# Pool values and output gates as Strassen units of the gates' pass, with the first head's elementwise work moved beside them

## The chip, the cores and the metric

The kernel runs on one core of a Trainium2 chip. Its engines are TensorE (PE in the profile; PEld is its weight load), VectorE (DVE), ScalarE (ACT), GpSimd (POOL) and SyncE (SP, which issues most DMA transfers in order). The metric is the time of one execution in device microseconds (us).

## What is computed

One layer of a decoder trunk, 1024 tokens and 16 meta tokens ahead of them (L = 1040 rows), width 1024, in float32. Cut to what matters here:

```python
u = rmsnorm(h, mix_norm_pre)
proj = u @ w_in                      # 4608 columns
q, f_logit, i_in, g_out, v_pool, gate_a, gate_b = split(proj)   # 512 x 5, 1024 x 2
a = hgrn2(q, f_logit, i_in, g_out)   # 4 heads of 128: recurrence in chunks, then rms norm, gain, * sigmoid(g)
p = multiscale_pool(v_pool)          # 4 groups of 128: trailing mean of 2, 4, 8, 16 rows minus the row,
                                     # times a 128 x 128 matrix, times a scale
z = sigmoid(gate_a) * (a @ w_branch_hgrn) + sigmoid(gate_b) * (p @ w_branch_pool)
h = h + rmsnorm(z @ w_out)
u = rmsnorm(h, ffn_norm_pre)
gt = causal_dwconv(u @ ffn_w_gate)
h = h + rmsnorm((gelu(gt) * (u @ ffn_w_up)) @ ffn_w_down)
```

In `hgrn2`, f = lb + (1 - lb) sigmoid(f_logit), k = (1 - lb) sigmoid(-f_logit), and b is the running sum of log f in a chunk.

## The kernel before

Features lie on the 128 partitions, tokens along the free axis. Every float32 product is made of three matmuls in a reduced type (float32r): the operands are split into a high and a low part (`hi` is a cast on ScalarE, `lo = x - hi` a subtraction on VectorE or GpSimd), and high x high, high x low, low x high are added in PSUM. So each weight block is loaded, cast and subtracted ahead of use (`wsplit`, `wsplit2`, and `ahead` of the Strassen class, lines 148 to 168 and 251 to 272).

There are two ways to make an output. A **projection** (`proj_parts`, line 197) makes one block of 128 output columns of w_in: 8 blocks along the contraction, 3 chunks of tokens, 3 products, 72 matmuls. It serves F (forget logits), Q, G (output gates), PV (pool values), and with fewer blocks PP (the pool's 128 x 128 matrix), BB and BA (the two branch products, 8 each, 4 blocks along the contraction). A **Strassen unit** (class `Strassen`, line 215) makes two such blocks over the two halves of the tokens with seven products P1 to P7 instead of eight. Each product has 4 blocks along the contraction and 3 matmuls for each; four products carry two extra columns (the halo) and are split into matmuls of 258 and 256 columns, three have 512. The halves of the moving operand and their sums (`b11`, `b21`, `b22`, `t1` to `t4`) are made once, before the pass; the weights' sums are made for every unit on GpSimd (`load_unit`). Results are added up on VectorE out of four PSUM pairs and handed to `put`.

The stages in order:

1. Norms, transposes and the projection of i (v of the heads), with the order of ScalarE, VectorE and TensorE written out by hand.
2. G of heads 0 and 1 (`EARLY_G = 2`), which covers the last of the Strassen sums; the results go through a sigmoid to DRAM (`gscr`).
3. **The gates' pass**: `gates.finish()` runs eight units for the columns of gate_a and gate_b; `put_gate` adds, applies the sigmoid and stores to DRAM (`sscr`). `load_unit` is called for the unit two ahead, behind P4.
4. **The heads' stage**: the string `ORDER` names the steps: F, Q, G, PV, PP, BB, BA are projections (a and b are halves of one), `c` is a head's forget chain (`chain_f`: scale, logarithm, scan), `h` the next part of `head_steps` of a head, `sp` the pool's mean and split, `sa` the split of a finished head, `w` a weight block of the FFN split ahead of time. `head_steps` makes, for six levels (2 to 64), a tile `d` from `b` (`level_in`: a subtraction, two Exp, products with q and with k), multiplies it with itself on TensorE and copies the masked result into the score tile (`level_out`); then `qs`, `kd`, `e1`, transposes, chunk states, output, norm, and the product with the output gate. The list `POOLED` names elementwise operations that run on GpSimd instead of VectorE.
5. BB and BA interleaved with the last of the heads, then w_out, norms, the FFN (a second Strassen pass of 22 units) and the down product.

Outside the parts written by hand, a planner orders each engine's instructions by the program's order and by when it thinks their inputs and tiles are there. Most tiles of stages 1 to 4 come out of one pool of 26 slots of 1088 floats per partition (`FM_SLOTS`, `LP`), so a tile can also wait for a slot. Sixteen slots hold the Strassen sums throughout stage 3.

## Time and profile before

| | |
|---|---|
| median of 3 runs | 1330.1 us (1330.08 to 1330.35) |
| time of the profiled execution | 1330.1 us |
| its span, first to last instruction | 1328.4 us |
| granted TensorE clock | 0.998 |
| DMA, mean over the span | 173 GB/s |

In a row of busy time by stretch the first two numbers are the stretch and its length; then, for each engine, busy time and number of instructions, the granted clock, the DMA engines' busy share and what they moved in GB/s. In a row of a timeline: start, duration, engine, line, operation, output and inputs, partitions and elements. In a row of a group: line, engine, operation, names, shapes, count, then busy time and mean duration in ns, then the idle time just before these instructions and what ended it. A row of waits names who waited, for whom, the sum, the number of times and the longest.

### The profile page before, as it was taken

What the parts mean: (1) busy time and instruction counts of PE and PEld (TensorE: products, weight loads), DVE (VectorE), ACT (ScalarE), POOL (GpSimd) and SP (SyncE); (2) the same over time, 40 slices, a digit from 0 to 9 for tenths busy, and PEclk for the clock granted to TensorE, in tenths of its full rate; (3) what the DMA queues carried; (4) which work ended last, traced back from release to release, by engine and by line L of the source; (5) the groups of instructions that cost most, each with busy time, mean ns of one, the idle gap of its engine ahead of it and who ended that gap; (6) DMA issues with size and microseconds to landing.
All of it is one profiled execution on the core that took longest, in us unless ns stands there. A gap on an engine that the chain in (4) does not pass through costs nothing.

```text
span 1328.4 us, 19923 instructions
## 1 busy us (share of the span) xinstructions
PE 1317.1 (99%) x7713; PEld 1177.6 (89%) x7713; DVE 970.7 (73%) x1229; ACT 566.8 (43%) x946; POOL 440.4 (33%) x327
## 2 busy tenths in 40 slices
PE   8999999999999999999999999999999999999997
PEld 7799899999999999987898888888888888888886
DVE  6765545389968777766578999888988885455758
ACT  5553333365556575235564222322222233444443
POOL 2015421226525720061025555545555652000000
PEclk9999999999999999999999999999999999999999
DMA  7134332411011157987686776676766799666644
GB/s 272 41 110 157 124 109 99 125 50 48 19 51 35 35 170 268 350 280 257 219 300 234 183 211 188 198 205 171 178 161 142 175 246 310 215 224 223 222 174 159
DMA packets 139665, 230.38 MB, mean 173 GB/s; under 512 B 9000, under 2 KB 77196, under 8 KB 139570
## 3 DMA queue, kind: packets, MB, share of 16 engines
q1 hardware_dynamic: 127506, 204.71, 45.3%
q0 software_dynamic: 12064, 24.38, 10.8%
q8 instruction: 61, 1.00, 0.3%
q14 instruction: 34, 0.28, 0.1%
HBM read 165.56 MB, written 86.53 MB: 190 GB/s over the span
## 4 chain that ended last, share of the span: by engine, by line
PE 95%; DVE 4%; DMA 0%; ACT 0%; issue 0%; SPq 0%; DVEq 0%
PE P L311 15%; PE P L312 15%; PE P L314 15%; PE pd L188 5%; PE pd L190 5%; PE pd L189 5%; PE pm L188 2%; PE pm L189 2%; PE pm L190 2%; PE sl L695 1%; PE ppv L208 1%; PE pbb L208 1%; PE ppv L212 1%; PE pbb L209 1%; PE ppv L209 1%; PE pbb L212 1%
## 5 line engine op out<-in xcount | busy, mean ns | idle before, releaser
L312 PE MATMUL P<-v,whi 128*128 128x512 f32 (+2 forms) x408 | 140.7, 353 | 0.0
L311 PE MATMUL P<-v,whi 128*128 128x512 f32 (+2 forms) x408 | 140.7, 352 | 0.0
L314 PE MATMUL P<-v,wlo 128*128 128x512 f32 (+2 forms) x424 | 135.1, 349 | 0.0
L1535 DVE TENSOR_TENSOR rot<-wraw,rot 128x1024 fp32r<-128x1024 f32 x31 | 38.0, 1225 | 72.3 <-ACT rot L1534 72.2
L282 POOL TENSOR_TENSOR swa<-wraw,wraw 128x512 f32<-128x512 f32 x28 | 42.3, 1510 | 133.0 <-DMA wraw<-in_ffn_w_gate_dram 69.3
L311 PEld LDWEIGHTS P<-v,whi 128*128 128x128 f32 x408 | 76.7, 188 | 10.4
L312 PEld LDWEIGHTS P<-v,whi 128*128 128x128 f32 x408 | 76.6, 188 | 10.2
L314 PEld LDWEIGHTS P<-v,wlo 128*128 128x128 f32 x424 | 74.0, 188 | 10.8
L256 ACT CAST whi<-wraw 128x512 fp32r<-128x512 f32 x78 | 46.1, 618 | 87.6 <-PE P L312 64.2
L190 PE MATMUL pd<-rot 128*128 128x512 f32 x272 | 82.1, 389 | 0.0
L189 PE MATMUL pd<-rot 128*128 128x512 f32 x272 | 82.1, 389 | 0.0
L188 PE MATMUL pd<-rot 128*128 128x512 f32 x272 | 81.1, 389 | 0.1
L1534 ACT CAST rot<-wraw 128x1024 fp32r<-128x1024 f32 x31 | 32.7, 1055 | 90.8 <-PE pd L190 89.4
L256 ACT CAST whi<-swa 128x512 fp32r<-128x512 f32 x56 | 33.4, 618 | 81.9 <-PE P L312 76.2
L1463 DVE SCALAR_TENSOR_TENSOR y<-g,par,y 128x1024 f32<-128x1024 f32 x44 | 64.5, 1467 | 0.8
L257 DVE TENSOR_TENSOR wlo<-swb,whi 128x512 fp32r<-128x512 f32 x56 | 59.9, 1075 | 6.9 <-ACT whi L256 6.9
L257 DVE TENSOR_TENSOR wlo<-wraw,whi 128x512 fp32r<-128x512 f32 x74 | 62.3, 864 | 2.7 <-ACT whi L256 2.7
L256 ACT CAST whi<-swb 128x512 fp32r<-128x512 f32 x56 | 33.4, 618 | 68.6 <-PE P L312 64.2
L188 PEld LDWEIGHTS pd<-rot 128*128 128x128 f32 x272 | 51.0, 188 | 11.1 <-DVE p L1471 0.5
L189 PEld LDWEIGHTS pd<-rot 128*128 128x128 f32 x272 | 51.1, 188 | 10.6
L190 PEld LDWEIGHTS pd<-rot 128*128 128x128 f32 x272 | 51.0, 188 | 10.6
L311 PE MATMUL P<-t4h,whi 128*128 128x258 f32 (+1 forms) x196 | 57.0, 307 | 0.0
(421 smaller groups left out, 4133.0 us busy)
## 6 DMA issues: line engine op xcount, KB each, us to landing
wraw<-in_w_in_dram SPq DMA_DIRECT2D x36, 512.0 KB, 4.0
yt<-ysum SPq DMA_DIRECT2D x33, 512.0 KB, 4.5
wraw<-in_ffn_w_gate_dram SPq DMA_DIRECT2D x26, 512.0 KB, 7.3
wraw<-in_ffn_w_up_dram SPq DMA_DIRECT2D x22, 512.0 KB, 6.1
wsum<-in_ffn_w_down_dram SPq DMA_DIRECT2D x22, 512.0 KB, 9.0
wraw<-in_w_out_dram SPq DMA_DIRECT2D x18, 512.0 KB, 5.5
ysum<-ys SPq DMA_DIRECT2D x11, 768.0 KB, 7.7
sa<-sscr SPq DMA_DIRECT2D x16, 513.0 KB, 6.8
```

What stands on the lines that cost most here:

```text
L188: pe.matmul(ps, ahi, bhi, start=first, stop=False)
L189: pe.matmul(ps, ahi, blo, start=False, stop=False)
L190: pe.matmul(ps, alo, bhi, start=False, stop=last)
L256: act.copy(hi, src)
L257: (pool_e if 4 <= i < 2 * self.early else dve).tensor_tensor(lo, src, rr(hi), ALU.subtract)
L282: pool_e.tensor_tensor(s1, a21, a22, ALU.add)
L311: pe.matmul(d, whi[:, k, :], xh[:, c : c + w], start=(k == 0 and onto is None), stop=False, **go)
L312: pe.matmul(d, whi[:, k, :], xl[:, c : c + w], start=False, stop=False, **go)
L314: pe.matmul(x[:, o : o + w], wlo[:, k, :], xh[:, c : c + w], start=False, stop=(k == 3), **go)
L1463: dve.scalar_tensor_tensor(a, g[:, j : j + SEQ], cvw[:, j, m : m + 1], a, ALU.mult, ALU.add)
L1534: act.copy(hi, src)
L1535: dve.tensor_tensor(lo, src, rr(hi), ALU.subtract)
```

## The change

- **Units.** The gates' pass gets four more units: G of all heads (units 8, 9) and PV of all groups (10, 11, which carry 16 extra columns, so that all 1040 rows come out). The halves of the moving operand grow from 514 to 528 columns. The units run in the order of `GATE_RUN`; `put_gate` stores sigmoid(G) in `sscr`, and PV's result goes to a tile.
- **Pooling in the pass.** Means, split and the 128 x 128 product of a group become a generator `pool_sums`, stepped by `GSTEPS` between the pass's products; the result goes to DRAM (`pscr`) and is read again by the steps `l0` to `l3`. PP and PV jobs and `sp` are gone.
- **Heads 0 and 1.** F0, Q0, F1, Q1 run where G0 and G1 ran (`FIRST_JOBS`); their sigmoids and q go to DRAM (`hscr0`). `prepare(h)` then does a head's elementwise work, a step at a time, and stores each part. `GSTEPS` has a character for every product of the pass: p is a step of `prepare`, t of a pool task, b both. It holds 32 p or b; a head has 22 steps, so the pass takes all of head 0 and ten of head 1; the other twelve are `p1` in `ORDER`. `head_steps` of both heads reads the parts.
- **Smaller edits.** The chain does its scaling on ScalarE and k's factor 1 - lb goes into q; the scan of heads 0 and 1 is made in nine pieces; the copies of levels 32 and 64 go to ScalarE, except one (`ON_ACT`); weights of the next unit are loaded behind P6 of the one before (`soon`); BB's results are stored and read again where more than four `h` steps follow (`SPILL`); v's meta rows are read from DRAM by every head; `ORDER` and `POOLED` are new; 27 slots of 1056 instead of 26 of 1088.

```diff
-EARLY_G = 2
+FIRST_JOBS = (("F", 0), ("Q", 0), ("F", 1), ("Q", 1))
-FM_SLOTS = 26
-LP = 1088
+FM_SLOTS = 27
+LP = 1056
+GS = HEADS
+V_UNIT = KD + GS // 2
+GATE_RUN = [0, 8, 1, 3, 2, 10, 9, 4, 11, 6, 5, 7]
...
+ORDER = ("p1 p1 p1 p1 h0 F2 p1 h0 p1 h0 p1 Qa2 p1 p1 p1 p1 p1 h0 h0 c2 h1 w1 Qb2 h0 w0 Fa3 h1 h0 h2 h0 h0 h2 w4 h1 "
+         "h0 h1 h1 h2 l0 Fb3 w4 c3 h1 h0 Q3 h0 h2 h2 h1 h3 h1 w4 l1 h2 h2 l2 l3 h1 h1 w2 h3 BB0 h2 h2 h3 h2 w5 BB1 "
+         "h3 h1 BB2 h3 BB3 w5 h1 h3 BB4 h3 h2 BB5 w3 sa1 h3 h3 h3 sa0 h2 BB6 h3 h1 w5 h2 BB7 sa2 w5 h3 sa3 BA1 BA5 "
+         "BA6 BA2 BA4 h3 BA0 BA3 BA7")
+POOLED = ("e1k.0 e1k.3 kdsub.2 lk32.1 lk4.1 lq32.1 lq64.3 lq8.0 osg.2 wBA2 wBA6 wBA7 wBB2 wF0 wF3 wPP2 wPV0 wPV1 "
+          "wQ0 qsmul.1 lq2.1 wQ2 sub2.3 lk32.3 lq4.2 sub8.0 lq32.0 lk64.1 sub8.3 lk2.1 qsmul.0 sub4.2 lq8.3 lq32.3 "
+          "lk16.1 lq2.0 lk8.1 sub32.2 lf.1 lq4.3 sub4.1 e1q.2 sub2.0 qsmul.3 lq4.0 lk8.3 sub64.1 lq8.2 lq4.1 sub2.2 "
+          "lk4.2 e1k.2 e1k.1 wQ3 kdsub.1").split()
+ON_ACT = "lo32.0 lo32.1 lo64.0 lo64.1 lo32.2 lo64.2 lo64.3".split()
+SPILL_OVER = 4
+GSTEPS = "p....pp.p.....pp...p...ptp.p.p.ppp.b.p..ttttbtttb.ttbbpbbttttbttbtttbb.tbt.bt.bppt.t"
...
             self.ahead(self.lead)
+            if self.steps:
+                c, self.steps = self.steps[0], self.steps[1:]
+                if c in "tb" and self.tasks:
+                    next(self.tasks[0], None) or self.tasks.pop(0)
+                if c in "pb":
+                    self.next_step()
...
-            return (0, 512 - HN // 2 - HALO, HT) if self.halo(u) else (HALO, 0, HN)
+            e = self.extra(u)
+            return self.most - e, (HN - e) // 4 * 2 if e else 0, HN + e
...
             dve.tensor_tensor(u2, u2, self.product(u, "P6"), ALU.add)
+            if load is not None and self.soon:
+                self.load_unit(load)
...
-        dve.tensor_scalar(f, f, oml[:, h : h + 1], lb[:, h : h + 1], ALU.mult, ALU.add)
-        dve.tensor_scalar(kk, kk, oml[:, h : h + 1], None, ALU.mult)
-        dve.tensor_scalar(f2, f, LUP, 1.0, ALU.mult, ALU.min)
-        dve.tensor_scalar(f2, f2, LOG_FLOOR * LUP, None, ALU.max)
+        act.activation(f2, f, AF.Identity, scale=omlu[:, h : h + 1], bias=lbu[:, h : h + 1])
+        act.activation(f, f, AF.Identity, scale=oml[:, h : h + 1], bias=lb[:, h : h + 1])
+        yield
+        dve.tensor_scalar(f2, f2, 1.0, LOG_FLOOR * LUP, ALU.min, ALU.max)
...
+    def prepare(h):
+        f = load_part("f", h)
+        yield True
+        kk, b, f2 = load_part("kk", h), slot(L, name="b"), slot(L, name="f2")
+        for _ in chain_steps(h, kk, b, f, f2):
+            yield True
+        del f2
+        nc.sync.dma_start(hpart("f", h), f)
+        q = load_part("q", h)
...
+        for lv in LEVELS:
+            d = slot(L, name="d")
+            for _ in level_steps(h, lv, d, q, kk, b):
+                yield True
+            nc.sync.dma_start(hpart(lv, h)[:, NM:], d[:, NM:L])
+        for z in ("qs", "kd"):
+            t = slot(L, name=z)
+            for _ in (qs_steps if z == "qs" else kd_steps)(h, t, q, kk, b):
+                yield True
+            lo = NM if z == "qs" else 0
+            nc.sync.dma_start(hpart(z, h)[:, lo:], t[:, lo:L])
...
     def put_gate(u, i, h, a, b, c=None):
+        if u >= V_UNIT:
+            if (u, i) not in vps:
+                vps[u, i] = slot(L, name="vp")
...
+    def whole_gate(u, i):
+        if u >= V_UNIT:
+            gates.tasks.append(pool_sums(2 * (u - V_UNIT) + i, vps.pop((u, i))))
...
-    gates = Strassen([(WIN, c + 2 * P * j) for c in (CA, CB) for j in range(KD // 2)], range(KD), EARLY, gq,
-                     lambda u: True, put_gate, lambda u, i: None)
+    gate_units = [(WIN, c + 2 * P * j) for c, n in ((CA, KD), (CB, KD), (CG, GS), (CV, HEADS)) for j in range(n // 2)]
+    gates = Strassen(gate_units, GATE_RUN, EARLY, gq,
+                     lambda u: NM if u >= V_UNIT else HALO, put_gate, whole_gate, NM)
...
+    gates.tasks = [load_ppw()]
+    gates.soon = True
     gates.finish()
```

More of the change, by code (lines that the diff above doesn't have):

```diff
@@ L225, in trunk_kernel, with __init__ @@
         SECOND = ("P3", "P5", "P7")
-        def __init__(self, units, run, early, quarters, halo, put, whole):
+        def __init__(self, units, run, early, quarters, extra, put, whole, most=HALO):
             self.units, self.run, self.early, self.bq = units, run, early, quarters
-            self.halo, self.put, self.whole = halo, put, whole
+            self.extra, self.put, self.whole, self.most = extra, put, whole, most
+            self.tasks, self.then, self.steps = [], [], ""
             self.raws, self.sums, self.p1s, self.halves = {}, {}, {}, {}
@@ L374, in rest @@
             x4 = self.product(u, "P4")
-            if load is not None:
+            if load is not None and not self.soon:
                 self.load_unit(load)
@@ L506, in warm @@
         for _ in range(n):
[L507 removed]
+            pe.matmul(junk_bank[:, :P], ones, ident, start=True, stop=True)
     wi = []
@@ new lines, in e1_steps, with all_of @@
+    def e1_steps(h, lf, q, kk):
+        e1 = slot(SEQ, name="e1")
+        lo2, q2, k2 = (t[:, NM:].rearrange("p (b two) -> p b two", two=2)[:, :, 1] for t in (lf, q, kk))
+        act.activation(e1[:, : SEQ // 2], lo2, AF.Exp)
+        act.activation(e1[:, SEQ // 2 :], lo2, AF.Exp, scale=-1.0)
+        yield
+        eng(f"e1q.{h}").tensor_tensor(q2, q2, e1[:, : SEQ // 2], ALU.mult)
+        eng(f"e1k.{h}").tensor_tensor(k2, k2, e1[:, SEQ // 2 :], ALU.mult)
+    def all_of(steps):
+        for _ in steps:
+            pass
@@ L1123, in trunk_kernel @@
         gates.load_first(3)
+        gates.steps = GSTEPS
+        gates.then = [prepare(h) for h in EARLY_HEADS]
         for e in range(0, EARLY, 2):
@@ L1173, in trunk_kernel @@
             continue
+        if kind == "p":
+            gates.next_step()
+            continue
         if kind == "h":
+            while i in EARLY_HEADS and len(gates.then) >= len(EARLY_HEADS) - EARLY_HEADS.index(i):
+                gates.next_step()
             if i not in gens:
```

403 lines of the change are left out of this document (248 added, 155 removed), and 3 rows, old and new, of the table ORDER.

## The prediction

> **What bounds the kernel now.** I read the busy times first, then busy time by stretch, TensorE's timeline for the pace of its matmuls, and last VectorE's groups where it is fullest.
>
> ```profile
> PE 1317.1 (99%) x7713; PEld 1177.6 (89%) x7713; DVE 970.7 (73%) x1229; ACT 566.8 (43%) x946; POOL 440.4 (33%) x327
> core 0: us, PE busy (x) PEld busy (x) DVE busy (x) ACT busy (x) POOL busy (x), PEclk, DMA share, GB/s
> 66.70:89.15 22.45, 22.45 (x145) 22.44 (x144) 17.86 (x38) 11.00 (x27) 0.00 (x0) 1.00 0.44 130
> 89.15:245.90 156.75, 156.75 (x1059) 145.51 (x1058) 76.78 (x112) 56.64 (x105) 56.15 (x40) 1.00 0.36 120
> 245.90:483.40 237.50, 236.93 (x1794) 232.97 (x1792) 185.13 (x201) 138.42 (x226) 107.44 (x53) 1.00 0.16 48
> 483.40:529.60 46.20, 46.20 (x301) 45.95 (x301) 34.37 (x57) 26.21 (x37) 2.42 (x1) 1.00 0.82 279
> 529.60:581.00 51.40, 51.40 (x327) 51.40 (x326) 37.67 (x65) 14.13 (x25) 7.01 (x4) 1.00 0.90 311
> 300.00:350.00 50.00, 49.56 (x408) 48.90 (x407) 49.61 (x42) 32.19 (x52) 34.50 (x18) 1.00 0.15 43
> 800.00:1100.00 300.00, 300.00 (x1657) 261.23 (x1656) 263.09 (x297) 86.84 (x141) 165.66 (x126) 1.00 0.73 186
> ```
>
> The stretches follow the kernel: the two early G projections (66.70), the gates' pass of eight Strassen units (89.15), heads with F, Q, G, PV and PP (245.90), BB (483.40), BA (529.60 to the first w_out matmul at 581.00). TensorE is busy in all of them, at a granted clock of 1.00; over 245.90 to 483.40 it is idle for 0.57 us. So a microsecond of matmul taken away is a microsecond of span, and there is nothing else to win; but whatever makes TensorE wait is paid in full.
>
> A busy row can hide waits, so the pace itself has to be seen:
>
> ```profile
> start us, us, engine line op out<-in xcount [idle before <-releaser]
> 66.70 0.32 PE L208 MATMUL pg<-uhi,whi 128*128 128x342 f32 x1
> 66.86 0.32 PE L209 MATMUL pg<-ulo,whi 128*128 128x342 f32 x1
> ...
> 89.15 0.28 PE L311 MATMUL P<-uhi,whi 128*128 128x258 f32 x1
> 89.27 0.28 PE L312 MATMUL P<-ulo,whi 128*128 128x258 f32 x1
> ...
> 115.05 0.39 PE L311 MATMUL P<-t1h,whi 128*128 128x512 f32 x1
> 115.28 0.39 PE L312 MATMUL P<-t1l,whi 128*128 128x512 f32 x1
> ...
> 245.88 0.32 PE L208 MATMUL pf<-uhi,whi 128*128 128x348 f32 x1
> 257.34 0.32 PE L208 MATMUL pq<-uhi,whi 128*128 128x342 f32 x1
> ```
>
> The second column overlaps the next row; the distance between starts is the cost: 0.16 us for 342 columns, 0.12 for 258, 0.23 for 512. Two G projections of 72 matmuls take 89.15 - 66.70 = 22.45 us, 11.23 each (0.156 a matmul). F0, shaped like a PV projection, takes 257.34 - 245.88 = 11.46. A Strassen unit, which makes two output blocks, takes 156.75 / 8 = 19.59.
>
> **The change on TensorE.** (1) Four G projections become two units: 4 x 11.23 - 2 x 19.59 = 5.74 us less. (2) Four PV projections become two units. These carry 16 extra columns instead of 2, so in four products of seven each matmul has 264 columns, 7 more than now on average: (0.156 - 0.12) / (342 - 258) x 7 = 0.003 us, times 96 matmuls 0.29. So 4 x 11.46 - 2 x (19.59 + 0.29) = 6.08 less. (3) PP: 36 matmuls x 0.156 = 5.6 before; after, four groups of six split matmuls and three whole ones, 4 x (6 x 0.12 + 3 x 0.23) = 5.6: nothing. (4) F0, Q0, F1, Q1 only move ahead of the gates: nothing. Together **11.8 us less**.
>
> Where the stages then lie: ahead of the gates 2 x (11.46 + 11.23) = 45.4 us instead of 22.45; the gates' pass 10 x 19.59 + 2 x 19.88 + 5.6 = 241.3 instead of 156.75; after it 335.1 (245.90 to 581.00) less eight F and Q (90.8) less G2, G3 (22.45), PV (45.84) and PP (5.6), plus F2, Q2, F3, Q3 (45.4), which is 215.8. The sum falls from 514.3 to 502.5. All that follows is untouched.
>
> **Who must keep up, in the gates' pass.** By the row of 89.15 a unit needs 9.6 us of VectorE, 7.1 of ScalarE, 7.0 of GpSimd in 19.59. Twelve units need 115 of VectorE. Added: head 0's level work by the groups below (4 x 1.68 + 2 x 1.20 + 6 x 0.89 = 14.5), some 16 for its other steps and its chain, 8 for the ten steps of head 1, 18 for the pooling (below). That is 172 of 241.3 us, 71%. The FFN's Strassen pass (800:1100) runs VectorE at 263.09 / 300 = 88% without a gap on TensorE, so I cost this at 0; without that cover, the same 18 us of pooling would be the loss. DMA: 18 more transfers of half a megabyte for the two heads and 8 for pooling are some 13 MB, 55 GB/s beside 120, still under the 186 of the FFN's pass: 0. A unit's weights are now asked for behind P6 of the unit before it, five products ahead of their first use, not twelve:
>
> ```profile
> wraw<-in_w_in_dram SPq DMA_DIRECT2D x36, 512.0 KB, 4.0
> ```
>
> Five products are some 14 us, two loads land in 4.0 to 8, and the split behind them works on half of what L155 does in 1.69 us (quoted below), so about 1 us on ScalarE and 1 on VectorE, an estimate: hidden, with 4 us to spare at the least; past that, every late unit stops TensorE, which is how the queue rival would cost.
>
> ScalarE mixes Exp and Ln steps with the gates' Sigmoid, and each alternation loads a table:
>
> ```profile
> 284.15 0.16 ACT L665 COPY scm<-sm 16x4 f32<-16x4 f32 x1
> 284.35 1.28 ACT L677 ACT_TABLE_LOAD   x1
> 285.64 0.64 ACT L677 ACTIVATE d<-d 128x512 f32<-128x512 f32 x1
> ```
>
> From the end of the copy (284.31) to the next instruction is 1.33 us. Some 15 groups of Exp or Ln at two loads each are 40 us, on 12 x 7.1 for the units and about 33 for the moved activations: 158 of 241 us, hidden. The Trainium skill (ScalarE: Activation LUTs, "What ACT_TABLE_LOAD costs") puts a switch at 1283 ns and a drain of some 1380 more. The trace agrees on the load and shows no drain behind it; with it the 15 groups would be 80 us and ScalarE 82% full, still hidden.
>
> **Who must keep up, behind the gates' pass.** Here cover is taken away: 335.1 us of matmuls become 215.8, and every BA product needs all four heads, so what the heads need of VectorE must fit into 215.8 - 45.2 (eight BA at 36 x 0.157) = 170.6 us. What it needs, by groups of now:
>
> ```profile
> L675 DVE TENSOR_TENSOR d<-b 128x1024 f32<-128x1024 f32 x20 | 32.8, 1678 | 1.1 <-ACT e L743 1.1
> L680 DVE TENSOR_TENSOR d<-d,kk 128x512 f32<-128x512 f32 x20 | 17.8, 891 | 0.1
> L679 DVE TENSOR_TENSOR d<-d,q 128x512 f32<-128x512 f32 x13 | 15.6, 1203 | 0.0
> ...
> L155 DVE TENSOR_TENSOR wlo<-wraw,whi 128x1024 fp32r<-128x1024 f32 x6 | 10.1, 1687 | 0.2 <-ACT whi L154 0.2
> L896 DVE TENSOR_TENSOR sa<-sa,pba 128x342 f32<-128x342 f32 x22 | 10.1, 506 | 10.7 <-PE pba L212 9.4 <-DMA sa<-sscr 0.8 <-PE pba L190 0.5
> ...
> L632 DVE TENSOR_TENSOR_SCAN b<-keep_on,f 128x1040 f32<-128x1040 f32 x4 | 9.3, 2325 | 0.2
> L1202 DVE TENSOR_TENSOR sa<-sa,sa 128x1026 f32<-128x1026 f32 x7 | 8.6, 1232 | 0.1
> L865 DVE TENSOR_TENSOR pll<-s,plh 128x1026 fp32r<-128x1026 f32 x4 | 7.0, 1743 | 0.6 <-ACT plh L864 0.6
> L872 DVE SCALAR_TENSOR_TENSOR plo<-ppp,par,phi 128x342 fp32r<-128x342 f32 x12 | 6.3, 567 | 0.0
> ...
> L631 DVE TENSOR_TENSOR f<-f,f 128x1040 f32<-128x1040 f32 x4 | 5.0, 1242 | 4.4 <-ACT f L630 4.4
> L859 DVE SCALAR_TENSOR_TENSOR s<-s,vp 128x1026 f32<-128x1026 f32 x4 | 4.9, 1221 | 1.8 <-POOL s L847 1.8
> L624 DVE TENSOR_SCALAR f<-f,oml,lb 128x1040 f32<-128x1040 f32 x4 | 4.6, 1141 | 13.4 <-ACT f L619 13.4
> ...
> L626 DVE TENSOR_SCALAR f<-f 128x1040 f32<-128x1040 f32 x4 | 3.9, 970 | 0.0
> ...
> L704 DVE COPY sc<-sl 32x256 f32<-32x256 f32 x8 | 3.3, 415 | 5.3 <-PE sl L691 5.2
> ...
> L625 DVE TENSOR_SCALAR kk<-kk,oml 128x1040 f32<-128x1040 f32 x4 | 3.0, 752 | 0.0
> ...
> L704 DVE COPY sc<-sl 64x512 f32<-64x512 f32 x4 | 2.7, 675 | 0.1
> ```
>
> Now it is busy 185.13 + 34.37 + 37.67 = 257.2 us. What leaves: pooling 7.0 + 6.3 + 4.9 = 18.2; five of six weight splits, 8.4; of the chain three instructions of every head (to ScalarE, or merged), 4.6 + 3.0 + 3.9 = 11.5, and two heads' scan and add, (9.3 + 5.0) / 2 = 7.1; levels, where the new engine list leaves VectorE nine instructions of each kind for heads 1 (from its third level on), 2 and 3: 66.2 - 9 x (1.68 + 0.89 + 1.20) = 32.3; the copies of the two widest levels, all but two now on ScalarE, 5.2. That is 82.7 less, 174.5 left, and 18.7 of it (L896 of pba, L1202) belong to BA's own time: **156 us of VectorE in 170.6**, 91%. Small steps of head 0 that I left out would lower it. Three edits I cost at 0 here: heads 0 and 1 read their parts, the pooled values and the meta rows of v from DRAM, where the row of 245.90 shows 48 GB/s and a DMA share of 0.16 (their first reader is an h step queued behind the p steps on VectorE, and F2's matmuls cover the landing); BB's results are stored and read again; the scan of heads 0 and 1 is cut into nine pieces ahead of time.
>
> Can it run at 91% while TensorE never waits? In 300:350 it ran at 99% and TensorE lost 0.44 us; in the FFN's pass at 88% with no loss. But over the whole of 245.90 to 483.40 it ran at only 185.13 / 237.50 = 78%, since chains leave it idle. Bounds: 0 at 99%; 156 / 0.78 - 170.6 = 29.4 at 78%. I take 90%, nearer the two rows where it had work in stock, for the planner can here choose among three heads, weight splits for the FFN and BB: 156 / 0.90 - 170.6 = **2.7 us**.
>
> The profiled execution has a time of 1330.1 us, 1.7 around its span of 1328.4; the median of the runs is also 1330.1. So 1330.1 - 11.8 + 2.7 = **1321.0**.
>
> **The rivals.** *No wait at all*: 1318.3. For it, the row of 300:350; against it, 91% is more than any long stretch shows.
>
> *VectorE becomes the bound behind the gates' pass*, and the kernel is slower: at the 78% of now the heads end 29.4 us late and BA with them: 1330.1 - 11.8 + 29.4 = 1347.7. It decides once its share falls below 156 / (170.6 + 11.8) = 85.5%; there the gain is gone.
>
> *SyncE's queue in the gates' pass.* It issues in order and mostly stands waiting:
>
> ```profile
> SPq L888 <- ACT sg L887: 83.1, 25, 6.9
> SPq L275 <- DVE wlo L257: 25.5, 8, 5.2
> ```
>
> These are 108.6 of 156.75 us; behind a store that waits for its sigmoid stand the next weights. About 26 more transfers, each holding the queue for 83.1 / 25 = 3.3 us, are 86; scaled to twelve units the old waits take 163 of 241, so 8 us would not fit: 1330.1 - 11.8 + 8 = 1326.3, and with tile slots that come free later the 1330 of no change. Against it: a wait that ends because its data come costs nothing while the next weights are four products ahead.
>
> **How the numbers follow.** Forecast 0.45, its own range 1318.5 to 1326; no wait 0.25; the queue 0.15 (0.06 a smaller gain, 0.05 no change, 0.04 slower); VectorE 0.15 (0.04 no change, where its share is near the 85.5%, and 0.11 slower, mostly short of the full price). A difference under 0.2%, 2.7 us, could not be told from none. Faster: 0.45 + 0.25 + 0.06 = 0.76; same: 0.05 + 0.04 = 0.09; slower: 0.04 + 0.11 = 0.15. The range reaches from just under the case of no wait, 1317, to 1335, about half of VectorE's price.
>
> **What would show it.** Right: the stretch from the first gate product to the first pf behind it is 241 to 245 us long, TensorE has no row of idle time before P, pg is gone and ppv is P; the time from there to the first w_out matmul is 216 to 222; VectorE is near 90% up to the first pba; idle time before pba or sl names VectorE, none longer than a few us. Wrong: idle time before P released by a DMA or by wlo (the queue), or a first pba preceded by tens of us with VectorE below 85%.

## The result and the profile after

The changed kernel takes **1341.66 us** (median of 6 runs, 1339.31 to 1347.07) beside 1330.24 for the kernel before on the same chip: a ratio of 1.0088, 95% interval 1.0068 to 1.0108. The forecast was 1321.0 and faster; the range ended at 1335. Measured twice more, each time beside the kernel before, it gave 1335.28, ratio 1.0043 (1.0028 to 1.0058), and 1334.91, ratio 1.0042 (1.0029 to 1.0056). So it is slower each time, by 4 to 11 us (0.4 to 0.9%, with 1 outside the interval each time), and what makes that spread is part of the answer.

Busy time by stretch, of the profiled execution (1341.08 us, span 1339.2). The columns are those of the rows in the prediction; 67.40 is the first of the early jobs, 113.70 the first product of the gates' pass, 357.30 the first pf behind it, 541.40 the first pba, 588.40 the first w_out matmul.

```profile
core 0: us, PE busy (x) PEld busy (x) DVE busy (x) ACT busy (x) POOL busy (x), PEclk, DMA share, GB/s
67.40:113.70 46.30, 45.66 (x290) 45.38 (x288) 22.31 (x49) 20.50 (x56) 0.00 (x0) 1.00 0.44 145
113.70:357.30 243.60, 243.37 (x1620) 223.95 (x1621) 178.13 (x226) 142.13 (x204) 127.98 (x79) 1.00 0.50 162
357.30:541.40 184.10, 177.23 (x1371) 171.91 (x1370) 132.98 (x169) 112.98 (x176) 62.11 (x38) 0.95 0.81 261
541.40:588.40 47.00, 46.23 (x293) 45.67 (x292) 34.97 (x56) 14.88 (x26) 7.00 (x4) 1.00 0.81 300
357.30:588.40 231.10, 223.45 (x1662) 217.59 (x1661) 167.95 (x224) 127.86 (x201) 69.11 (x42) 0.96 0.81 269
357.30:400.00 42.70, 39.77 (x270) 38.85 (x269) 28.16 (x20) 26.73 (x39) 28.43 (x18) 0.88 1.01 320
...
371.60:381.80 10.20, 9.40 (x41) 9.40 (x42) 3.57 (x5) 6.59 (x13) 2.81 (x2) 0.50 1.06 382
381.90:450.00 68.10, 66.41 (x564) 64.82 (x563) 53.00 (x60) 46.65 (x73) 20.74 (x13) 1.00 0.83 282
450.10:456.90 6.80, 5.76 (x61) 5.61 (x62) 6.38 (x10) 6.74 (x14) 1.85 (x1) 0.50 0.96 236
```

Against the forecast's lengths, the early jobs took 46.3 us (45.4), the gates' pass 243.6 (241.3), the heads' stage 231.1 (215.8). What lies ahead grew by 0.7, and what follows, w_out to the end, from 747.4 to 750.8 (1328.4 - 581.0 and 1339.2 - 588.4). The excess is 0.7 + 0.9 + 2.3 + 15.3 + 3.4 = 22.6 us, and -11.8 + 22.6 = +10.8 is the growth of the span from 1328.4 to 1339.2. Two thirds of it sit in the heads' stage. There the row shows three things at once: TensorE idle for 231.10 - 223.45 = 7.65 us, a granted clock of 0.96, and a DMA share of 0.81 where the kernel before had 0.16 over most of the stage. Right behind the gates' pass the DMA engines are full: 1.01.

TensorE's timeline of the changed kernel shows what belongs together (start, duration, engine, line, operation, names, shapes, idle time before and what ended it):

```profile
369.04 0.63 PE L222 MATMUL pf<-uhi,wlo 128*128 128x348 f32 x3
371.14 0.25 PE L808 MATMUL sm<-rq,em 128*16 128x2 f32 x4 [1.47 <-DMA rq<-hscr]
372.40 7.09 PE L833 MATMUL sl<-r 128*128 128x64 f32 x32 [1.00 <-DMA r<-hscr]
...
380.54 0.49 PE L218 MATMUL pq<-uhi,whi 128*128 128x342 f32 x1
380.82 0.49 PE L219 MATMUL pq<-ulo,whi 128*128 128x342 f32 x1
...
382.22 0.32 PE L218 MATMUL pq<-uhi,whi 128*128 128x342 f32 x1
382.38 0.32 PE L219 MATMUL pq<-ulo,whi 128*128 128x342 f32 x1
...
447.73 1.06 PE L879 MATMUL pt<-ident,rkd 128*128 128x128 f32 x8 [0.60 <-DMA rkd<-hscr]
448.63 0.27 PE L882 MATMUL pt<-ident,rkd 128*16 128x128 f32 x1
451.14 2.97 PE L829 MATMUL sl<-d 128*32 128x32 f32 x48 [2.23 <-DVE d L757]
```

F2's matmuls run out before head 0's parts have come from DRAM: 1.47 us idle for q, 1.00 for a level. From 371.60 the clock stands at 0.50 for 10.2 us, and the pq matmuls start 0.28 us apart instead of 0.16. The second place is at 449: head 1's transposes wait for kd, then head 2's level for VectorE, and from 450.10 the clock is 0.50 again for 6.8 us. Both stretches are multiples of 3.41 us by the clock's records (10.24 and 6.83). What they cost shows beside a later execution of the same program without half clock (the row of 357:581 below): TensorE was busy there for 216.96 us, here for 223.45, so 6.5 us. With the 7.65 idle that is 14.1 of the stage's 15.3; the rest, 217.0 against 215.8, is the matmuls' own.

Of the idle time in the stage, 3.9 us end with a DMA (q, a level, kd, the pooled values) and 3.7 with VectorE or ScalarE. In two later profiles of the same program it is 3.1 and 4.2, then 1.7 and 5.2. So transfers are a part of the waiting, and the chains of elementwise work are as large a part.

Why q came late: SyncE's queue, and some of the issues with their median time from issue to landing, over 357 to 590:

```profile
360.38 4.12 SPq L691 DMA_DIRECT2D rq<-hscr  x1
364.59 0.38 SPq L691 DMA_DIRECT2D r<-hscr  x1
```

```profile
sa<-sscr SPq DMA_DIRECT2D x16, 513.0 KB, 8.5
r<-hscr SPq DMA_DIRECT2D x12, 512.0 KB, 7.1
sb<-sscr SPq DMA_DIRECT2D x7, 513.0 KB, 9.4
vh<-vscr SPq DMA_DIRECT2D x4, 512.0 KB, 8.1
```

In the kernel before, over 246 to 483, `vh` landed in a median of 5.3 us, and `sa` in 6.8 in its own full stretch; here they take 8.1 and 8.5. Not every transfer is slow: `sg` lands in 4.7. The issue of rq alone holds the queue for 4.12 us. In the two later profiles it holds it for 3.22 and 2.77, and there TensorE doesn't wait for q, only for the level behind it (1.00 and 0.74 us).

The wait for `d` at 451 is of another kind. ScalarE's timeline:

```profile
441.32 1.42 ACT L679 ACTIVATE q<-pq,oml 128x342 f32<-128x342 f32 x3 [1.46 <-PE pq L222]
442.75 1.28 ACT L939 ACT_TABLE_LOAD   x1
444.05 1.42 ACT L939 ACTIVATE rs<-ms,eps_t 128x342 f32<-128x342 f32 x3
445.49 1.28 ACT L753 ACT_TABLE_LOAD   x1
446.78 0.63 ACT L753 ACTIVATE d<-d 128x512 f32<-128x512 f32 x1
447.32 0.61 ACT L754 ACTIVATE d<-d 128x512 f32<-128x512 f32 x1
```

Head 2's Exp stands behind head 0's norm, with a table load on either side of it, 2.56 us of loads on the chain that TensorE waits for. VectorE's products follow at 447.44 and the matmul at 451.14. ScalarE idles for 1.46 us until Q3's last matmuls are done, and then works without a break: 9.72 of the 9.80 us from 441.30 to 451.10, VectorE 7.42. So for these 10 us it is full, though over the whole stage it is busy for only 127.86 of 231.10 us. No run takes the table loads or the norm out of that place, so this reading rests on the timeline.

### The profile page after: what moved, and what is told of

Its sections match the earlier page's. It is cut to its first block, busy times and chain, and to the rows that moved or that the text cites. A ratio compares the mean times of both kernels' runs of the same rounds, so it can differ in the third digit from the quotient of the medians.

```text
span 1339.2 us, 20195 instructions
## 1 busy us (share of the span) xinstructions
PE 1319.1 (98%) x7665; PEld 1166.1 (87%) x7665; DVE 991.3 (74%) x1260; ACT 610.5 (46%) x985; POOL 466.2 (35%) x348
## 2 busy tenths in 40 slices
DMA packets 149217, 277.83 MB, mean 207 GB/s; under 512 B 10536, under 2 KB 74700, under 8 KB 149122
## 3 DMA queue, kind: packets, MB, share of 16 engines
q0 software_dynamic: 12064, 24.38, 10.8%
## 4 chain that ended last, share of the span: by engine, by line
PE 88%; DMA 5%; ACT 2%; DVE 1%; issue 1%; POOL 1%; SPq 1%; DVEq 0%; POOLq 0%; ACTq 0%
PE P L322 16%; PE P L325 16%; PE P L323 16%; PE pd L198 5%; PE pd L200 5%; PE pd L199 5%; PE sl L833 2%; PE pm L199 2%; PE pm L200 2%; PE pm L198 2%; DMA wraw<-in_w_out_dram 2%; DMA sb<-sscr 1%; PE pv L199 1%; PE pv L200 1%; PE pv L198 1%
## 5 line engine op out<-in xcount | busy, mean ns | idle before, releaser
L267 ACT CAST whi<-wraw 128x512 fp32r<-128x512 f32 x90 | 53.0, 618 | 81.7 <-PE P L323 68.4
L268 DVE TENSOR_TENSOR wlo<-wraw,whi 128x512 fp32r<-128x512 f32 x86 | 80.5, 958 | 12.7 <-ACT whi L267 12.7
L293 POOL TENSOR_TENSOR swa<-wraw,wraw 128x512 f32<-128x512 f32 x32 | 50.0, 1564 | 111.2 <-DMA wraw<-in_ffn_w_gate_dram 74.6
L323 PEld LDWEIGHTS P<-v,whi 128*128 128x128 f32 x408 | 76.6, 188 | 10.3
L268 DVE TENSOR_TENSOR wlo<-swb,whi 128x512 fp32r<-128x512 f32 x64 | 71.6, 1125 | 9.0 <-ACT whi L267 9.0
L267 ACT CAST whi<-swa 128x512 fp32r<-128x512 f32 x64 | 38.1, 616 | 76.6 <-PE P L323 71.0
L322 PE MATMUL P<-uhi,whi 128*128 128x258 f32 (+2 forms) x240 | 69.0, 304 | 0.6 <-ACT q L679 0.6
L267 ACT CAST whi<-swb 128x512 fp32r<-128x512 f32 x64 | 38.2, 617 | 67.4 <-PE P L323 63.5
L323 PE MATMUL P<-ulo,whi 128*128 128x258 f32 (+2 forms) x240 | 68.9, 305 | 0.0
L322 PE MATMUL P<-t2h,whi 128*128 128x258 f32 (+2 forms) x228 | 65.3, 304 | 0.2 <-DVE sg L1022 0.2
L322 PE MATMUL P<-t4h,whi 128*128 128x258 f32 (+2 forms) x228 | 64.9, 302 | 0.1
```

The costliest lines, as they stand in the source:

```text
L267: act.copy(hi, src)
L268: (pool_e if 4 <= i < 2 * self.early else dve).tensor_tensor(lo, src, rr(hi), ALU.subtract)
L293: pool_e.tensor_tensor(s1, a21, a22, ALU.add)
L322: pe.matmul(d, whi[:, k, :], xh[:, c : c + w], start=(k == 0 and onto is None), stop=False, **go)
L323: pe.matmul(d, whi[:, k, :], xl[:, c : c + w], start=False, stop=False, **go)
```

## The experiments

The expectations call the layout of tiles A (alignment first, then the stride, A2) and the waits and transfers behind the gates' pass B. Ratios are against the kernel before on the same chip.

### Layout: slots of 1056 floats

512-column matmuls start 0.2267 us apart on average in the gates' pass of before and 0.2311 after (mean over 280 and 429 pairs of neighbours). This distance is called the pitch below. Two kernels add 64 bytes ahead of the pools, to the changed kernel and to the one before:

```diff
+    pad = const.tile([P, 16], F32, name="pad")
+    pool_e.memset(pad, 0.0)
```

> The changed kernel with one more constant tile of 64 bytes per partition, so that all large tiles lie 64 bytes further on (at multiples of 128 bytes, as in the kernel before); nothing else differs. Theory A (part of the loss is the tiles' place in memory: 512-column matmuls of the gates' pass start 0.231 us apart after the change and 0.227 before): the mean distance falls to 0.227, the gates' pass is about 2 us shorter, the whole time about 4 to 5 us, from 1341.7 to about 1337. Rival (the slower matmuls come from the added transfers or VectorE work): no change in the distance, 1341.7.

> The kernel before with the same tile of 64 bytes, which puts its large tiles 64 bytes off a multiple of 128. Theory A: its 512-column matmuls in the gates' pass go from 0.227 to about 0.231 us apart and the time rises by 4 to 5 us, to about 1334.5. Rival: 1330.2 as before.

The pitch stayed at 0.2311 and 0.2267; the times are 1336.15, ratio 1.0039 (1.0025 to 1.0052), and 1330.41, ratio 1.0000 (0.9992 to 1.0009). A shift by 64 bytes does nothing to the pitch. That the time still came out at the first expectation's 1337 is luck: the kernel with no edit gave 1335 in both later measurements. Next the stride, in the kernel before (`U0 = LP - L` follows it: the rows begin 16 floats into their part of the two large tiles, not 48):

```diff
-LP = 1088
+LP = 1056
```

> The kernel before with tile slots of 1056 instead of 1088 floats per partition, nothing else. Theory A2 (the slower 512-column matmuls come from the slots' stride, which puts rows at other places in the memory): matmuls of the gates' pass go from 0.227 to 0.231 us apart and the time rises by 4 to 5 us to about 1334.5. Rival (it comes from the added work, transfers or instructions): 0.227 and 1330.2.

1335.31 us, ratio 1.0034 (1.0021 to 1.0047), pitch 0.2301 in the gates' pass. Its stretches:

```profile
67.50:90.10 22.60, 22.60 (x146) 22.60 (x145) 17.62 (x38) 11.01 (x27) 0.00 (x0) 1.00 0.43 129
90.10:247.90 157.80, 157.80 (x1057) 145.57 (x1056) 76.50 (x112) 56.72 (x104) 55.86 (x40) 1.00 0.36 119
247.90:583.50 335.60, 334.74 (x2419) 330.23 (x2418) 257.80 (x320) 178.77 (x287) 116.04 (x58) 1.00 0.36 120
```

A full clock, the same order of work, and the span is 1333.2 instead of 1328.4. The 4.8 us are spread: 0.8 ahead of the first row, 0.15, 1.05, 0.5 in the rows, 2.3 behind. The 0.8 is a wait of 0.74 us at 7.7 that the profile of before doesn't have, while one of the changed kernel has it too (1.36 us). The other 4.0 are put down to the stride; the medians are 4.4 apart. Scaled to the longer gates' pass of the changed kernel (1.05 x 243.6 / 156.75 = 1.6 in place of 1.05) the 4.0 become some 4.6 us there, an estimate. The pitch shows it; the rows only say that TensorE is busy.

The obvious remedy is the old stride, with one slot less so that it fits:

```diff
-FM_SLOTS = 27
-LP = 1056
+FM_SLOTS = 26
+LP = 1088
```

> The changed kernel with tile slots of 1088 floats again and 26 of them, as in the kernel before; the order of the engines' work is almost the same. Theory A2 (the stride of 1056 costs some 5 us over the whole kernel): matmuls of the gates' pass 0.227 us apart, the gates' pass 241.3 us, the time about 5 us under e5's 1335.3, so about 1330.5. Rival (the 27th slot is needed): transfers are asked for later, more idle time behind the gates' pass, 1336 or more.

The pitch came back (0.2276, without eight of 428 pairs that ran at half clock), and the time went up to 1352.42, ratio 1.0156 (1.0140 to 1.0172). Its waits of TensorE and its gates' pass:

```profile
PE P L322 <- DVE plo L983: 3.5, 1, 3.5
PE sl L829 <- DVE d L757: 3.4, 1, 3.4
PE P L322 <- ACT e L779: 2.5, 1, 2.5
```

```profile
113.00:367.00 254.00, 245.46 (x1620) 226.23 (x1621) 178.82 (x226) 142.61 (x205) 129.05 (x80) 0.99 0.47 156
```

TensorE idles for 8.5 us in the pass and waits for head 0's and the pool's elementwise work. The likely reason is the missing 27th slot, without which that work can't run as far ahead. So the faster stride is bought with a slot, and here the slot is worth more. Between the two, the stride of 1088 for the two large tiles alone, which hold the high and the low part of the normed input:

```diff
-U0 = LP - L
+UP = 1088
+U0 = UP - L
...
-        return upool.tile([P, n], dtype, tag="u", name=nm(name), padded_shape=[P, KD * LP])
+        return upool.tile([P, n], dtype, tag="u", name=nm(name), padded_shape=[P, KD * UP])
```

> The changed kernel with 1088 floats per row only in the two large tiles that hold the normed input's parts, and 27 slots of 1056. If the stride of these tiles decides, the first stage's matmuls (their weights come from these tiles) are 0.227 us apart again and the time is 1 to 3 us under e5; if the slots' place decides, only those products of the gates' pass that read the large tiles change, or none.

1335.79, ratio 1.0040 (1.0028 to 1.0053); the gates' pass 242.3 us, pitch 0.2302. To take the chip out of the comparison, the changed kernel and this one ran again side by side:

> The changed kernel itself, as the base for the two runs beside it on one chip. Earlier chips gave 1.0088 and 1.0043 of the kernel before; both theories expect between these.

> Only the two large tiles of the Strassen halves at a stride of 1088 floats, 27 slots of 1056 kept. If the stride of what TensorE reads is worth what the shorter matmul pitch in that kernel's gates' pass says (243.6 down to 242.3 us, and 0.5 ahead of it), it is 1.5 to 3 us faster than the changed kernel on the same chip; if the earlier difference was the chip's or that of the half-clock stretches, less than 1 us.

1334.91, ratio 1.0042 (1.0029 to 1.0056), and 1337.03, ratio 1.0040 (1.0026 to 1.0054). The gain of 1 to 2 us that the pitch shows can't be told in the time.

### The half clock, and the waits behind the gates' pass

The changed kernel once more, with no edit:

> The changed kernel once more, so that the others are compared on one chip. Both theories: 1341.7 within 3 us, two stretches of half clock between 357 and 470 us.

1335.28, with one stretch of half clock (3.41 us) instead of two. The later run side by side (1334.91) had none in its profiled execution; its busy time by stretch, gates' pass and heads' stage:

```profile
113.60:356.90 243.30, 242.98 (x1619) 223.76 (x1620) 179.57 (x226) 142.69 (x205) 128.27 (x79) 1.00 0.50 162
357.00:581.00 224.00, 216.96 (x1663) 210.73 (x1661) 167.45 (x223) 127.38 (x201) 70.44 (x42) 1.00 0.80 277
```

The stage is 224.0 us, 7 us less than in the first profile, with nearly the same idle time (7.04). So half clock, not more waiting, makes the difference between these two. Over the 19 executions of this kernel, the eight with a mean clock of 0.997 or more average 1334.7 us, the nine at 0.994 or less 1341.7. So most of the spread between the three measurements goes with the half clock. But even the execution without any half clock has a span of 1331.9, 3.5 above before.

Can the waits be covered? First, by putting all of Q2 ahead of head 0's matmuls:

```diff
-ORDER = ("p1 p1 p1 p1 h0 F2 p1 h0 p1 h0 p1 Qa2 p1 p1 p1 p1 p1 h0 h0 c2 h1 w1 Qb2 h0 w0 Fa3 h1 h0 h2 h0 h0 h2 w4 h1 "
+ORDER = ("p1 p1 p1 p1 h0 F2 Qa2 Qb2 p1 h0 p1 h0 p1 p1 p1 p1 p1 p1 h0 h0 c2 h1 w1 h0 w0 Fa3 h1 h0 h2 h0 h0 h2 w4 h1 "
```

> The changed kernel with the whole of Q2 ahead of head 0's first matmuls, so that TensorE has 11 us of work while head 0's parts land; three p1 steps move with it. Theory B (head 0's parts come late from DRAM at the end of the gates' pass, TensorE stands 2.8 us and then runs at half clock for 10.2 us): both go, 2.8 + 5.1 = about 8 us, 1341.7 to about 1334; granted clock 1.00 from 366 to 382 us. Rival (VectorE or the engines as a whole are behind, the gap only moves): the time stays within 3 us of 1341.7.

1343.19, ratio 1.0092 (1.0079 to 1.0105), beside 1336.15 of the padded kernel on the same chip. The wait for q moved from 371 to 403 us and grew to 2.6, and the one for `d` grew from 2.2 to 5.7. The Q2 matmuls covered nothing, because the steps behind them became later as well.

Second, to keep the clock up, 15 matmuls on constants behind F2:

```diff
+        if kind == "j":
+            fill = bank("pj")
+            for _ in range(15):
+                pe.matmul(fill[:, :P], ones, ident, start=True, stop=True)
+            continue
...
-ORDER = ("p1 p1 p1 p1 h0 F2 p1 h0 ...
+ORDER = ("p1 p1 p1 p1 h0 F2 j0 p1 h0 ...
```

> The changed kernel with 15 matmuls on constants (about 3 us, result unused) between F2 and head 0's first matmuls. They end no wait. Theory C (the half clock follows from TensorE being idle for some 3 us): the clock stays at 1.00 there and the time falls by about 5 us although work was added, to about 1337. Rival (the clock drops for another reason, as the load of the other engines or of DMA): the clock drops at the same place and the time stays or rises, 1341.7 to 1345.

TensorE's timeline and stretches in that run:

```profile
369.71 3.51 PE L1339 MATMUL pj<-ident,ones 128*128 128x128 f32 x30
373.15 0.25 PE L808 MATMUL sm<-rq,em 128*16 128x2 f32 x4
373.34 3.79 PE L833 MATMUL sl<-r 128*128 128x64 f32 x32
```

```profile
369.00:382.00 13.00, 13.00 (x104) 12.86 (x103) 5.20 (x5) 9.77 (x16) 8.31 (x5) 1.00 1.05 379
441.10:454.70 13.60, 13.60 (x95) 12.94 (x95) 12.62 (x16) 10.86 (x18) 2.84 (x2) 0.50 0.70 221
```

The 32 matmuls of sl take 3.79 us instead of 7.09 and the clock is 1.00, with the DMA share as high as before. One execution doesn't show it, since other executions have no half clock here without a fill either. Over all profiles that have these steps behind F2, none of three with a fill shows half clock there, and six of twelve without do, at a DMA share of 0.99 to 1.10 over the 13 us around that place in each. So full transfers alone don't bring the half clock, and idle time is the likely cause. The fill replaces the wait and doesn't end it: the time is 1338.64, ratio 1.0055 (1.0043 to 1.0067), no better than the padded kernel's 1336.15 on the same chip, and a gap of 1.93 us at 439 is followed by 13.65 us of half clock. Filling both places, with the large tiles at 1088:

```diff
-... h0 Q3 h0 h2 h2 h1 h3 h1 ...
+... h0 Q3 h0 h2 h2 j0 h1 h3 h1 ...
```

> As the run beside it, with 15 matmuls on constants behind F2 and 15 more ahead of head 1's steps behind Q3, where TensorE waits. If idle time costs mainly through the half clock that follows it, the clock stays at 1.00 over 360 to 460 us and the kernel is 3 to 5 us faster than the one beside it, about 1331. If each wait has its own cause that comes later anyway, the half clock moves behind another gap and the time stays within 2 us or gets longer.

1339.71, ratio 1.0068 (1.0056 to 1.0080), slower than the kernel beside it (1337.03). A gap of 1.96 us at 437 names ScalarE's `rh`, and 13.65 us of half clock follow. With 26 slots of 1088, Q3 was moved four steps back in one kernel, and both fills were put into another:

```diff
-... h0 Q3 h0 h2 h2 h1 h3 h1 ...
+... h0 h0 h2 h2 h1 Q3 h3 h1 ...
```

> e9 with Q3 behind head 2's next step and one of head 1, so that its 11 us of matmuls stand where TensorE waits near 445 us. Theory B (what is left of the loss is short waits behind the gates' pass, where too little matmul work is ready, each followed by half clock): the wait and the half clock near 445 go, 3 to 6 us less than e9, to about 1326, under the kernel before. Rival (the heads are late as a whole): the wait moves to another place, same time as e9.

> e9 with 15 matmuls on constants (about 3 us each time, result unused) behind F2 and another 15 behind head 2's step after Q3. They end no wait. Theory C (idle time costs twice, by the half clock that follows): no half clock between 357 and 470 us, 2 to 5 us less than e9, about 1327. Rival: no gain, 1330 to 1334.

1359.01, ratio 1.0216 (1.0202 to 1.0230), and 1355.77, ratio 1.0188 (1.0175 to 1.0202), against 1.0156 without either edit. In each of these runs TensorE waits for the next chain instead, and none is faster than the kernel without the edit.

### Slots, transfers, VectorE, and dividing the heads

BB's results kept in slots, not stored and read again:

```diff
-SPILL_OVER = 4
+SPILL_OVER = 99
```

> The changed kernel with BB's results kept in their slots, no store to DRAM and no second load: 14 transfers of half a megabyte less between 460 and 590 us. Theory B (the transfers behind the gates' pass are what TensorE waits for): the DMA share from 460 to 588 falls, BA's stretch and the first w_out matmuls lose their waits, 2 to 4 us less, to about 1338; the gaps near 370 and 450 stay. Rival (the tile slots are the limit): the kept results hold eight slots, loads are asked for later, and the time rises above 1342.

1347.50, ratio 1.0123 (1.0110 to 1.0136). TensorE waits once for 10.3 us, and the DMA share over 460 to 540 us falls to 0.48 (its waits, then that stretch):

```profile
PE sl L829 <- POOL d L757: 10.3, 1, 10.3
```

```profile
460.00:540.00 80.00, 69.22 (x513) 67.37 (x513) 48.47 (x77) 37.09 (x57) 16.39 (x11) 0.91 0.48 152
```

Beside 1335.28 on the same chip that is 12 us more, with fewer transfers and the same work on the engines (VectorE 990.2 us, 991.3 in the first profile). So the stores of BB pay for themselves. A slot for `d` that comes free too late, as the rival had it, is not what the trace names: GpSimd's wait for `d` ends with ScalarE's Exp, and ScalarE stood still for 3.98 and 5.11 us ahead of two weight casts in front of it, first until a store of another weight was done, then until a load came. Why these are late is open.

Transfers in the other direction: eight copies of half a megabyte within DRAM at the start of the heads' stage (large tiles at 1088):

```diff
+    extra = dram.tile([8, P, TQ], F32, name="extra")
+    for i in range(8):
+        nc.sync.dma_start(extra[i], sd[14 + i % 2])
```

> e10 with eight added copies of half a megabyte from DRAM to DRAM at the start of the heads' stage (result unused), 8.4 MB read and written. At the 320 to 340 GB/s seen there they are some 13 to 25 us of transfers. Theory B: the time rises by 8 us or more, to 1344 or more, with TensorE waiting for heads' parts. Rival (transfers have room): up to 3 us more.

1349.62, ratio 1.0151 (1.0136 to 1.0166), beside 1.0040 without them (on another chip): some 15 us. TensorE's longest wait and the heads' stage in the profiled execution, the slowest of four (1353.07):

```profile
PE sm L809 <- DMA rq<-hscr: 7.2, 1, 7.2
```

```profile
355.30:601.20 245.90, 230.60 (x1662) 224.60 (x1661) 163.21 (x224) 128.22 (x201) 67.42 (x42) 0.92 0.79 270
```

They stand in front of head 0's q, whose wait grows to 7.2 us; idle time doubles to 15.3 us (6.95 without them), and 37.55 us run at half clock. Moving the FFN's weight splits, whose loads share the queue, to later places, most of them behind BB0, should then help:

```diff
-... c2 h1 w1 Qb2 h0 w0 Fa3 h1 h0 h2 h0 h0 h2 w4 h1 h0 h1 h1 h2 l0 Fb3 w4 c3 h1 h0 Q3 h0 h2 h2 h1 h3 h1 w4 l1 ...
+... c2 h1 Qb2 h0 Fa3 h1 h0 h2 h0 h0 h2 h1 h0 h1 h1 h2 l0 Fb3 c3 h1 h0 Q3 h0 h2 h2 h1 h3 h1 l1 ...
```

> e10 with the FFN's weight blocks that are split ahead of time moved behind BB0: about 7 MB of loads and stores, and 10 us of VectorE, leave the first 90 us behind the gates' pass. Theory B (the transfers there set the pace: DMA share 0.89 to 1.0): the share from 357 to 446 us falls to about 0.7, the waits near 370 and 445 shrink, the time falls by 4 us or more, to 1331 or less. Rival (chains of VectorE and ScalarE in heads 0 to 2): less than 2 us.

It doesn't: 1341.14, ratio 1.0091 (1.0074 to 1.0108). At the start of the stage it does what was expected, though the DMA share over 357 to 400 stays at 1.03: TensorE idles for 0.29 us there instead of 0.87, and the clock is 1.00 instead of 0.92. Over 400 to 440 the share falls from 0.74 to 0.58. But the waits at 440 (4.3 us for `d`) and 552 (4.4 for `sa`) name VectorE, and both are longer than without the edit (1.6 and 1.1). So the transfers ahead of head 0's parts seem to decide the wait at the start of the stage, and chains of ScalarE and VectorE the later ones.

VectorE's share itself, with 20 added sums of 512 columns (a median of 0.69 us each; VectorE is busy for 15.8 us more in the stage). The edit, and the row of the stage:

```diff
+    scr = const.tile([P, 512], F32, name="scr")
+    pool_e.memset(scr, 0.0)
+    added = []
...
+            if len(added) < 20 and "v" in heads[i]:
+                added.append(dve.tensor_tensor(scr, heads[i]["v"][:, :512], scr, ALU.add))
```

> The changed kernel with 20 added VectorE additions of 512 columns (0.7 us each, 14 us in all) behind the first 20 steps of the heads (result unused). Theory B: VectorE has room (72% busy), up to 4 us more, 1339 at most. Rival (VectorE is the bound behind the gates' pass, as one rival of the prediction had it): 10 us or more, 1345 or more.

```profile
357.60:590.40 232.80, 221.33 (x1663) 215.66 (x1661) 183.78 (x245) 128.16 (x202) 70.96 (x42) 0.98 0.78 268
```

1344.10, ratio 1.0102 (1.0087 to 1.0117). The stage is 232.8 us at 79% VectorE, with 11.5 idle. Against the 1.0042 and 1.0043 above that is some 8 us, against the first 1.0088 almost nothing, so the size is not settled; it lies between the two forecasts. A full VectorE would have cost all of the 15.8; the result fits chains with little other work in stock better, but doesn't settle it.

Last, only head 0 moved ahead (F1 and Q1 back in the stage, with an order put together by hand and not tuned):

```diff
-FIRST_JOBS = (("F", 0), ("Q", 0), ("F", 1), ("Q", 1))
+FIRST_JOBS = (("F", 0), ("Q", 0))
...
-ORDER = ("p1 p1 p1 p1 h0 F2 p1 h0 p1 h0 p1 Qa2 p1 p1 p1 p1 p1 h0 h0 c2 h1 w1 Qb2 h0 w0 Fa3 h1 h0 ...
+ORDER = ("h0 F1 h0 c1 Q1 h0 h1 h0 F2 h0 h1 c2 Qa2 Qb2 h1 w1 h0 w0 Fa3 h1 h0 ...
```

> The changed kernel with only head 0 beside the gates; F1, Q1 and head 1's work go behind the pass as in the kernel before, 26 transfers of half a megabyte less and 22.7 us more matmuls to cover VectorE, which gets some 26 us of work there. Theory B (transfers and the waits on them): DMA share from the end of the gates' pass to the first w_out matmul falls from 0.81 to about 0.65, no half clock or one short stretch of it, and the time falls to 1320 to 1328, under the kernel before. Rival (VectorE is the bound behind the pass): moving head 1's work back makes it later, the time rises to 1345 or more.

1360.83, ratio 1.0224 (1.0210 to 1.0237). The DMA share of its stage is 0.59, and it waits 8.4 us for `po <- st` and runs 37.5 us at half clock. With fewer transfers it is slower, so taking transfers away does not help when elementwise work comes back in their place; how much of the loss is the untuned order stays open.

No kernel tried was faster than the one before.

## Why the prediction was wrong

**The failed step** is "three edits I cost at 0 here", and with it two prices that have no term at all: the half clock behind a wait, and the stride. The cover named for the three edits was the row of 245.90, with 48 GB/s and a DMA share of 0.16. That is the stage as it was before the change put transfers into it and took a third of its length away. The whole kernel moves 277.83 MB instead of 230.38; from the end of the gates' pass to w_out it was 40.17 MB in 335.1 us, 120 GB/s, and is 62.88 MB in 233 us, 270 GB/s. The prediction even names what saves the first read: F2's matmuls. They cover some 12 us; the queue takes 4.12 to issue q, in the stretch where the DMA share is 1.01, and in the first profile q came 1.47 us late. Waits that end with a DMA come to 3.9 us of the stage there, and to 3.1 and 1.7 in the two later profiles. The reads were set beside the bytes of the old stage, and never turned into bytes per microsecond of the shorter one.

**The price of a wait** was missing as well. The prediction takes a stall at its length. In the first profile 7.65 us idle brought another 6.5 of half clock. The Trainium skill (TensorE: Matmul & The Clock Gate, "Part 1: The HAM clock gate") says the clock halves after an idle window of about 3.4 us and comes back after a busy one, with free-running windows. The trace agrees on the half and on the unit (10.24, 6.83 and 3.41 us), but no gap in the first profile was as long as 3.4 us. Behind F2, far less was enough in one execution and not in another of the same program, that with the large tiles at 1088: 0.84 us of idle time was followed by the first of these rows, 0.99 by the second (the stretch 371.70 to 378.50 of its two profiles).

```profile
371.70:378.50 6.80, 6.80 (x28) 6.80 (x28) 4.93 (x5) 4.50 (x7) 3.97 (x2) 0.50 1.05 390
```

```profile
371.70:378.50 6.80, 6.80 (x49) 6.80 (x49) 5.14 (x5) 4.70 (x8) 3.77 (x2) 1.00 1.03 402
```

The first made 28 matmuls in 6.80 us, the second 49. The clock's records show what differs. In each of the 20 profiles every change of the clock lies on a grid of 3.413 us, the full stretches between included (365.23, 68.27 and 880.64 us in the first profile are 107, 20 and 258 units), and the grid starts at another place in every execution. In the slow one of these two a unit began at 368.25, ahead of the gap's end at 368.70, so it held idle time and then only narrow matmuls; in the other one a unit began at 369.34, behind the gap's end at 369.05. That fits windows that add up such idle time and narrow matmuls, but how much is enough is open.

**The layout** was seen in the diff, listed among the smaller edits, and given no term. With 4.0 to 4.4 us in the kernel before it is worth most of the units' gain on G (5.74).

**VectorE behind the gates' pass**, 156 us in 170.6, was mis-sized. VectorE's total in the stage was right, 167.95 against 174.5, but what it does in BA's own time is 34.97, not 18.7 (the prediction's own row of 529.60 has 37.67), and 132.98 are left in 184.1 us: 72%, not 91. The +2.7 that came of it is not far below the idle time that ends with VectorE or ScalarE, 3.7 us in the first profile and 4.2 and 5.2 in the later ones; that it is of this size is luck, since it was worked out for an engine at 90%. The rival that put VectorE as the bound below a share of 85.5% had the sign, the low share, and a time (1347.7) some 6 us above the first measurement and 12 to 13 above the later ones. Its price rests on the 156 us as well: with the work measured, its 78% would cost nothing (133.0 / 0.78 = 170.5). What it did see is that chains leave engines idle. ScalarE got no term behind the gates' pass at all, and the longest wait of the stage in the first profile stands behind its norm and its table loads.

**What held.** TensorE's work: 217.0 us at full clock in the heads' stage against 215.8; 46.3 against 45.4; the gates' pass 243.6 against 241.3, most of whose excess is the stride's (about 1.6). The units are worth what was worked out for them, within 2.3 us. Everybody kept up in the gates' pass: 0.23 us idle, VectorE 178.13 us (172 forecast), ScalarE 142.13 (158). The queue rival fell there:

```profile
SPq L1026 <- ACT sg L1025: 68.0, 31, 5.0
SPq L286 <- DVE wlo L268: 47.0, 14, 14.5
```

SyncE's queue waits for these 115 of the pass's 243.6 us, less than the 163 that the rival scaled up from 108.6, and no product behind the first is late (the first waits 0.64 us for ScalarE's q). That cover is thin: with 26 slots TensorE waits in the pass. "All that follows is untouched" was wrong by 3.4 us, of which 2.3 appear with the stride alone. "No wait" fell: of the three profiled executions of the changed kernel the quietest still idles for 7.04 us in the stage.

In that execution the sum is: 1328.4 - 11.8 = 1316.6; some 4.6 for the stride, 7.0 idle; 1328.2 of 1331.9, with 3.7 not accounted for. In the first profile 0.6 more of idle time and 6.5 of half clock come on top, 1335.3 of 1339.2, with 3.9 open. Against the forecast's span, 1316.6 + 2.7 = 1319.3, the 19.9 us too many of the first profile are 6.5 of half clock, some 4.6 of stride, 3.9 of waits that end with a DMA, 1.0 more than the 2.7 of waits that end with VectorE or ScalarE, and 3.9 that stay open.

## What to carry to other kernels

Cost a transfer at the share its stage will have after the change, bytes added and length taken away together, never at the share that a row of before shows; and where TensorE's first work behind a full stage is fed from DRAM, ask what is in flight in the microseconds ahead of it. Compare the distance between starts of equal matmuls whenever a tile's size changes, since busy rows can't show a slower pace. Once TensorE stalls, by half a microsecond already in one run here, count the half clock that may follow, which nearly doubled the price of the stalls in the first profile. And look at every engine that a chain passes through where the cover is taken away, since a mean share of 55% hid 10 us in which ScalarE was full.

## What the runs showed of the hardware

The **stride of what TensorE reads** changes its pace: 512-column matmuls start 0.2267 us apart on average with tiles of 1088 floats and 0.2301 with 1056 in the same kernel, 1.5% more, and 0.2276 again in the changed kernel at 1088. A shift of 64 bytes changes nothing. Which property of the stride does it is open; no other stride was tried, and the places of the rows in the tiles move with it.

**The half clock comes in units of 3.41 us** (3.41 to 23.89 in a row over all runs), on a grid that starts at another place in every execution, behind gaps of about 0.5 to 10 us, and not behind every one: 3.01 us at 459 in the run with added sums had none behind it. It makes single executions of one program differ by up to 13 us (1333.85 to 1347.07 over 19), where the kernel before, without gaps of more than 0.6 us on TensorE behind its first stage, stayed between 1329.97 and 1334.08 over 65.
